# Where modulation sums and token sums stand in the engines' order, and the last down projection by latent then context columns

## The chip, the cores and the metric

One NeuronCore of a Trainium2 chip runs the whole program. The metric is the device time of one execution in microseconds (us): the median over the runs, and beside it the time of one execution recorded by the hardware profiler. The engines are TensorE (PE in the profile; PEld is its weight load), VectorE (DVE), ScalarE (ACT), GpSimd (POOL) and SyncE (SP), whose queue issues the transfers from memory. Each engine executes its instructions strictly in one order.

## The reference

A diffusion transformer with two layers, 512 latent tokens and 256 context tokens of width 1024. Each layer's norms are modulated by vectors that come from a condition: six chunks of 1024 for each layer, for latents and for context.

```python
for i in range(DEPTH):                       # 2
    mod_l = silu(c) @ ada_w[i] + ada_b[i]    # 6 x 1024: shift, scale, gate (mixer), shift, scale, gate (FFN)
    mod_c = silu(c_ctx) @ ada_w[i] + ada_b[i]
    hn = rms_norm(h, norm_mix_w[i]) * (1 + sc1) + sh1
    y = attention(hn) if i == 0 else hgrn2(hn)
    h = h + gt1 * y
    hn = rms_norm(h, norm_ffn_w[i]) * (1 + sc2) + sh2
    a, u = split(hn @ ffn_w_in[i])           # 1024 x 5632
    h = h + gt2 * ((silu(a) * u) @ ffn_w_out[i])     # 2816 x 1024
    # the context goes the same way, in layer 0 only; in layer 1 it only feeds the mixer
return rms_norm(h, final_norm_w)
```

Everything is float32.

## The kernel before, in words

**Tiling.** The tokens lie along the free dimension: `hT[k]`, k = 0 to 7, holds 128 features by 768 tokens, columns 0 to 511 latents and 512 to 767 context. A product of two float32 matrices is done as three matmuls of rounded parts, `mm3` (L113, L114, L115: high by high, high by low, low by high). So each operand is split first: `split` takes the high part on ACT (L89) and the low part on DVE (L92), unless another engine is named. Tiles of weights come through a ring of raw, high and low tiles; a load (L850 for the FFN) waits until a raw tile of the ring is free.

**Order.** The program text is Python that emits instructions; a scheduler then fixes the order of each engine by modelled readiness and cost. What an engine meets at run time is that fixed order, with waits on semaphores. All loads go through SP's one queue, in order too.

**Layer-0 FFN** (`ffn`, about 424 to 983 us in the profile). The hidden dimension is 22 tiles of 128. Tiles 0 and 1 are multiplied plainly, tiles 2 to 21 by a scheme that takes 7 instead of 8 block products over the two halves (384) of the token columns: the units m1, m2, m5, m6, m4, m3, m7 of `pair_units`. Their results are combined by DVE (L1008, L1035, L1043) and ACT (L1002, L1036). A product's PSUM bank is free for the next when its combination or copy has read it. The down projection is summed into `hT` in five parts of 5, 5, 4, 4, 4 hidden tiles, each with eight output tiles o (`fo_units`, `fo`). For each o there is a latent run (128x512) and a context run (128x256) of matmuls, and `residual` (L679, DVE) adds each run's bank, times its gate, to `hT`. In the last part `fo_out` also sums the squares of the new `hT` over k (`sumsq_add`: squares on ACT L270, additions on DVE L271) for the next norm. `LATE = 4`: for o of 4 and more of the last part the context runs are held back until all latent runs are done, and the weights of those o lie in tiles of their own (`fot1`, `fot3`). Between the context runs `norm_tail` makes the norm's factor for the latents: column sums on PE (L277), scale and power (L279 DVE, L281 POOL), and the broadcast (L287 DVE, L291 PE).

**Modulation sums.** `ada_acc` forms one chunk of the modulation as a matrix-vector product on DVE: for each half of 512 columns, eight loads of 128x512 weights (tile `adw`, L218), one product (L237) and seven accumulations (L239) by a column of the activated condition, for each of nv columns (2 with context, 1 without), then a transpose (L245) and a reduction (L246), and at the end a small matmul and addition (L253, L254). It is a generator: `fill.step(n)` takes it n yields further, so the place of the calls sets where in the program text its instructions stand. In the layer-0 FFN `ada_mix` runs chunks 0 and 1 of layer 1 (two steps after each down-projection unit); chunks 2, 3 and 4 run in the HGRN heads with `wide=True` (loads of two tiles at once, the sum in `acc_n`), one step at each scan step. Chunk 5 runs in the layer-1 FFN.

**Passage to the mixer.** `modulate` makes the normed and modulated tiles for k = 0 to 7, for the latents and, three k later, for the context: a DVE product with the norm's factor (L311) into a temporary `mtmp` (two buffers), the high part on ACT (L312), the low part on DVE for even k (L314), on ACT and POOL for odd k (L317). A copy of the scan masks (L1417, DVE) follows it.

**HGRN heads** (1012 to 1480 us). Each of eight heads runs projections (`hg`, `hz`, `hq`, `hv`) as fill between the steps of a log-depth scan (`scan_head`: L1481 and L1482 on POOL, L1504, L1534, L1541 on DVE, L1509, L1527 on PE). Then the layer-1 FFN, `ffn_plain`, runs to the end.

## Time and profile before

| | us |
|---|---|
| median of 3 runs | 1883.21 (1881.03 to 1883.71) |
| the profiled execution | 1879.18 |
| its span | 1877.3 |
| PE busy | 1792.3 (95%) |
| DVE busy | 1231.6 (66%) |
| ACT busy | 765.4 (41%) |
| POOL busy | 531.7 (28%) |

A row of the profile's groups gives line, engine, operation, output and inputs by the program's names, with the busy time and mean duration. A row of waits gives the engine and line that waited, whom it waited for, the total in us, the number of waits and the longest. In a row of the timeline the bracket at the end is the engine's idle time just before and what ended it. A row of busy time by stage gives the window, its length, and for PE, PEld, DVE, ACT and POOL the busy time with the number of instructions, then PE's granted clock, the share of the transfer engines and GB/s.

### The profile page before, as it was taken

The page shows a single profiled execution, that of the slowest core. Times are in us where ns is not written, and L with a number is a line of the kernel's source. Part 1 is how long each engine was busy: PE and PEld are TensorE (multiplying, and loading weights), DVE is VectorE, ACT ScalarE, POOL GpSimd, SP SyncE. Part 2 cuts the span into 40 slices and gives each one's busy share as a digit, 9 for nine tenths or more (in the row PEclk, how much of TensorE's full clock was granted, in tenths as well). Part 3 has the DMA queues.
Part 4 walks back from the last instruction along what each step waited for, and adds up shares of the span by engine and source line. Part 5 has one row for each costly group of instructions (what it writes and reads, how often), then busy time and mean ns, then how long its engine had stood idle before and what let it go on. Part 6 is the DMA issues. An engine that isn't in the chain of part 4 may idle for free.

```text
span 1877.3 us, 30240 instructions
## 1 busy us (share of the span) xinstructions
PE 1792.3 (95%) x11929; PEld 1632.8 (87%) x11929; DVE 1231.6 (66%) x2104; ACT 765.4 (41%) x1465; POOL 531.7 (28%) x501
## 2 busy tenths in 40 slices
PE   8989999999899999999999989999998999999998
PEld 6778688888789989999988889888897799898997
DVE  3676688888996646664676675676648774344443
ACT  4434777776433525252435233223233332232224
POOL 1244355445313313131314253434535200000000
PEclk9999999999999999999999999999999999999999
DMA  9433410002243122312232422232111243323331
GB/s 324 166 114 97 161 36 24 24 3 66 63 138 92 58 73 62 107 57 79 63 121 64 127 85 73 80 102 90 57 57 34 86 152 94 97 87 94 91 91 55
DMA packets 212942, 166.40 MB, mean 89 GB/s; under 512 B 7441, under 2 KB 189889, under 8 KB 212801
## 3 DMA queue, kind: packets, MB, share of 16 engines
q1 hardware_dynamic: 212512, 163.43, 28.5%
q8 instruction: 94, 1.54, 0.3%
q10 hardware_dynamic: 288, 1.05, 0.1%
q14 instruction: 48, 0.39, 0.1%
HBM read 162.36 MB, written 2.10 MB: 88 GB/s over the span
## 4 chain that ended last, share of the span: by engine, by line
PE 71%; DVE 15%; ACT 4%; DMA 4%; POOL 3%; issue 2%; SPq 0%; POOLq 0%; DVEq 0%; ACTq 0%
PE ffo L114 5%; PE ffo L115 5%; PE ffo L113 5%; PE ffi L113 4%; PE ffi L114 4%; PE ffi L115 4%; PE pt L706 3%; DMA adw<-in_ada_w_dram 2%; PE lv L1527 2%; PE x L115 2%; PE x L113 2%; PE x L114 2%; DVE QD L1534 2%; PE sc L648 2%; PE hz L114 1%
## 5 line engine op out<-in xcount | busy, mean ns | idle before, releaser
L114 PE MATMUL ffi<-fnl,whi_fi 128*128 128x256 f32 x704 | 198.0, 281 | 1.1 <-DVE fnl L1219 1.1
L113 PE MATMUL ffi<-fnh,whi_fi 128*128 128x256 f32 x704 | 198.8, 283 | 0.1
L115 PE MATMUL ffi<-fnh,wlo_fi 128*128 128x256 f32 x704 | 197.8, 281 | 0.0
L679 DVE SCALAR_TENSOR_TENSOR hT<-ffo,modc,hT 128x512 f32<-128x512 f32 (+1 forms) x106 | 66.8, 637 | 121.6 <-PE ffo L115 121.3
L114 PEld LDWEIGHTS ffi<-fnl,whi_fi 128*128 128x128 f32 x704 | 133.2, 189 | 1.7 <-DVE fnl L1219 1.5
L113 PEld LDWEIGHTS ffi<-fnh,whi_fi 128*128 128x128 f32 x704 | 132.7, 189 | 0.4 <-issue 0.3
L115 PEld LDWEIGHTS ffi<-fnh,wlo_fi 128*128 128x128 f32 x704 | 132.8, 189 | 0.0
L1534 POOL TENSOR_TENSOR KD<-KD,tot 128x384 f32<-128x384 f32 x96 | 106.2, 1130 | 75.5 <-ACT kc L1517 73.9
L281 POOL TENSOR_TENSOR rc<-rc,mhalf 128x2 f32<-128x2 f32 (+2 forms) x7 | 6.3, 902 | 395.9 <-DVE rc L279 395.9
L113 PE MATMUL ffo<-gh,whi_w 128*128 128x512 f32 (+1 forms) x320 | 107.6, 340 | 2.6 <-ACT gh L89 2.6
L696 POOL TENSOR_SCALAR pf<-pf,st 128x768 f32<-128x768 f32 (+1 forms) x96 | 73.6, 769 | 126.7 <-DVE st L695 90.2
L114 PE MATMUL ffo<-gl,whi_w 128*128 128x512 f32 (+1 forms) x320 | 108.7, 340 | 0.3 <-DVE gl L92 0.3
L115 PE MATMUL ffo<-gh,wlo_w 128*128 128x512 f32 (+1 forms) x320 | 108.9, 341 | 0.0
L89 ACT CAST whi_fi<-raw_fi 128x1024 fp32r<-128x1024 f32 x44 | 46.2, 1051 | 148.4 <-PE ffi L114 70.2
L1517 ACT COPY kc<-KD 128x256 f32<-128x256 f32 x112 | 42.8, 413 | 114.6 <-PE lv L1527 49.4
L92 DVE TENSOR_TENSOR ptl<-pt,pth 128x384 fp32r<-128x384 f32 (+1 forms) x160 | 79.8, 524 | 12.4 <-ACT pth L89 11.2
L89 ACT CAST pth<-pt 128x384 fp32r<-128x384 f32 (+1 forms) x160 | 69.9, 461 | 34.4 <-PE pt L706 22.7
L692 DVE TENSOR_REDUCE st<-sc 128x1 f32<-128x768 f32 (+1 forms) x96 | 74.2, 773 | 13.9 <-PE sc L649 11.1
L694 ACT ACTIVATE pf<-sc,st 128x768 f32<-128x768 f32 (+1 forms) x96 | 73.4, 765 | 19.2 <-DVE st L692 18.3
L113 PE MATMUL hz<-hnh,whi_hz 128*128 128x512 f32 (+1 forms) x224 | 78.6, 351 | 0.0
L1527 PE MATMUL lv<-QD,kc 128*128 128x128 f32 x448 | 65.2, 290 | 13.1 <-DVE QD L1534 8.9
L706 PE MATMUL pt<-ident,pf 128*128 128x128 f32 x448 | 72.2, 275 | 5.2 <-DVE ptl L92 3.9
(724 smaller groups left out, 5953.6 us busy)
## 6 DMA issues: line engine op xcount, KB each, us to landing
adw<-in_ada_w_dram SPq DMA_DIRECT2D x56, 512.0 KB, 4.0
raw_fi<-in_ffn_w_in_dram SPq DMA_DIRECT2D x44, 512.0 KB, 3.7
adw<-in_ada_w_dram SPq DMA_DIRECT2D x48, 256.0 KB, 2.9
raw_hz<-in_hgrn_w_in_dram SPq DMA_DIRECT2D x14, 512.0 KB, 3.8
raw_fo<-in_ffn_w_out_dram SPq DMA_DIRECT2D x16, 448.0 KB, 3.7
adr<-in_ada_w_dram SPq DMA_DIRECT2D x16, 256.0 KB, 4.4
adr<-in_ada_w_dram SPq DMA_DIRECT2D x8, 512.0 KB, 6.8
raw_wq<-in_attn_w_qkv_dram SPq DMA_DIRECT2D x8, 512.0 KB, 6.3
```

The costliest lines, as they stand in the source:

```text
L89: ACT.copy(hi, src)
L92: (eng or DVE).tensor_tensor(lo, src, hi.bitcast(F32), op=ALU.subtract)
L113: PE.matmul(ps, ahi, bhi, start=first, stop=False, **kw)
L114: PE.matmul(ps, ahi, blo, start=False, stop=False, **kw)
L115: PE.matmul(ps, alo, bhi, start=False, stop=last, **kw)
L679: DVE.scalar_tensor_tensor(hT[o][:, a:e], ps, mcol(layer, ch, o, v), hT[o][:, a:e], op0=ALU.mult, op1=ALU.add)
L692: DVE.tensor_reduce(st3[:, 0:1], ps[:, :nk], op=ALU.max, axis=AX.X, negate=True)
L694: ACT.activation(pf, ps[:, :nk], AF.Exp, bias=st3[:, 0:1], accum_out=st3[:, 1:2])
L696: POOL.tensor_scalar(pf, pf, st3[:, 2:3], 1.0, op0=ALU.mult, op1=ALU.mult)
L706: PE.transpose(pt[:, i * P : (i + 1) * P], pf[:, (i0 + i) * P : (i0 + i + 1) * P], ident)
L1527: PE.matmul(ps[:, cs], kc[:, cs], mv, start=True, stop=True)
L1534: eng.tensor_tensor(view, view, f, op=ALU.mult)
```

## The change

**Modulation sums.** In layer 0's FFN now chunks 0 to 3 are summed, in the HGRN heads only chunk 4, from head 1 on and at every third step. A narrow sum loads three tiles ahead (three buffers, before two); the yield that stood between a sum's first loads and its first product is gone; the transposed tile lies in the slot of `sw`. Steps are taken one at each pair unit m5 and three at each down-projection unit of parts 0 to 3 (before, two at each unit of all five parts and none at the pair units); for o > 0 two of the three stand between the latent and the context run. `pin` (`tc.keep_in_program_order`) holds the marked instructions of an engine in the order of the program text relative to their neighbours there: the products, accumulations and transposes of the sums, POOL's subtractions for the FFN's operands, and the masks copy.

**Last down projection.** All eight latent runs, then all eight context runs. The weights of o of 2 and more lie in tiles of their own. The squares are added on DVE for latents and on POOL for context. The norm's factor for the latents is made in the context runs of o = 2 and o = 4.

**Norm behind it.** The modulated tiles lie in slots that FFN operands left (`hnp`), and four temporaries (before, two) in the slot of one more operand; none of these slots is read by the last down projection. The masks copy stands behind the first pair of projections.

```diff
-LATE = 4
+    pin = tc.keep_in_program_order
-    def ada_acc(layer, ch, nv, fp, wide=False):
+    def ada_acc(layer, ch, nv, fp, wide):
...
-                raw = spare(f"adw{layer}{ch}{hf}{k}")
+                raw = fp.tile([P, 512], F32, tag="adraw", bufs=3, name=f"adw{layer}{ch}{hf}{k}")
...
-            raws = [load(hf, 0), load(hf, 1)]
-            yield
+            ahead = 2 if wide else 3
+            raws = [load(hf, i) for i in range(ahead)]
...
-                        DVE.scalar_tensor_tensor(a, raw, cc, a, op0=ALU.mult, op1=ALU.add)
-                    if v == nv - 1 and k + 2 < KT:
-                        raws.append(load(hf, k + 2))
+                        pin(DVE.scalar_tensor_tensor(a, raw, cc, a, op0=ALU.mult, op1=ALU.add))
+                    if v == nv - 1 and k + ahead < KT:
+                        raws.append(load(hf, k + ahead))
...
-            POOL.tensor_tensor(b11, b11, b12, op=ALU.subtract)
+            pin(POOL.tensor_tensor(b11, b11, b12, op=ALU.subtract))
...
-            POOL.tensor_tensor(b12, b22, b12, op=ALU.subtract)
+            pin(POOL.tensor_tensor(b12, b22, b12, op=ALU.subtract))
...
-                sumsq_add(acc_n[:, a:e], fp, hT[o][:, a:e], o, o == 0, tag="adraw", width=512)
+                sumsq_add(acc_n[:, a:e], late_pool[0], hT[o][:, a:e], o, o == 0, POOL if v else DVE,
+                          tag=f"g{8 + (o + v) % 2}", bufs=1, width=n)
...
-            if p_ == len(parts) - 1 and o >= LATE:
+            if p_ == len(parts) - 1:
                 held.append((o, g))
                 runs = [(o, g, spans[0])]
                 if o == KT - 1:
...
                 for (v, a, e), p in zip(spans, ps):
                     fo_out(p_, o, p, v, a, e)
+                fill.step(2)
                 return
             for (v, a, e), p in zip(spans, ps):
                 fo_mm(p_, g, p, a, e, range(nj))
                 fo_out(p_, o, p, v, a, e)
+                if v == 0:
+                    fill.step(2)
...
-                units.append(dict(own=None, w=512, after=after, src=src, pe=lambda g, fn=fn: fn(j, g), steps=0, done=done))
+                units.append(dict(own=None, w=512, after=after, src=src, pe=lambda g, fn=fn: fn(j, g), steps=int(i == 2), done=done))
...
-                if p_ == len(parts) - 1 and o >= LATE:
-                    own = ("t1", "t3")[(o - LATE) // 3], (o - LATE) % 3 * 512
+                if p_ == len(parts) - 1 and o >= 2:
+                    own = ("t1", "t3")[(o - 2) // 3], (o - 2) % 3 * 512
...
-                                  pe=lambda g, o=o: fo(p_, o, g), steps=2, done=("fo", p_, o)))
+                                  pe=lambda g, o=o: fo(p_, o, g), steps=int(p_ < len(parts) - 1), done=("fo", p_, o)))
...
-        for ch in range(2):
+        for ch in range(4):
             fill.add(ada_ffn(1, ch, fp))
...
-        if o == LATE + 1:
+        if o == 2:
             rst1.append(rstd_cols(fp, acc_n[:, :NL], NL))
-        elif o == KT - 1:
-            rst1[0] = rstd_psum(fp.tile([P, 512], F32, tag="adraw", bufs=2, name="dg"), rst1.pop(), NL)
+        elif o == 4:
+            rst1[0] = rstd_psum(fp.tile([P, T], F32, tag="g8", bufs=1, name="dg"), rst1.pop(), NL)
...
-    hi, lo = hn_tiles(hp)
+    hi, lo = [], []
+    for m in ("b11", "b21", "t4", "b22"):
+        for c, ts in (("h", hi), ("l", lo)):
+            t2 = hnp.tile([P, 2, T], F32R, tag=f"x{m}{c}", name=f"hn{m}{c}")
+            ts += [t2[:, 0], t2[:, 1]]
...
-    modulate(hp, hT, rst1, "mix", 1, hi, lo, SP2, ctx_rstd)
+    turns = [0]
+    mts = [hnp.tile([P, 2, T], F32, tag=f"xt2{c}", name=f"mt{c}") for c in "hl"]
...
+    modulate(mtmp, hT, rst1, "mix", 1, hi, lo, SP2, ctx_rstd)
...
-    DVE.tensor_copy(masks, mraw)
...
+    pin(DVE.tensor_copy(masks, mraw))
+    afill = Fill()
+    afill.add(ada_ffn(1, 4, hp, True))
     tail = None
-    afill = Fill()
-    for ch in (2, 3, 4):
-        afill.add(ada_ffn(1, ch, hp, True))
...
-            afill.step(1)
+            if h and i % 3 == 1:
+                afill.step(1)
...
-        if h == 1:
-            while len(afill.gens) > 2:
-                afill.step(1)
```

The lines of the changed kernel lie a little lower in number: L92 is L91 there, L239 is L235, L1035 is L1033, L1043 is L1041, L679 is L676. First DVE's order around the combination L1035 of hidden tile 3, at the start of the FFN; `adacc` is a modulation sum, `wlo_w` the low part of a weight tile. Before:

```order
L239 SCALAR_TENSOR_TENSOR adacc_6401<-adw_6537,csil,adacc_6401 128x512
L239 SCALAR_TENSOR_TENSOR adacc_6402<-adw_6537,csil,adacc_6402 128x512
L92 TENSOR_TENSOR wlo_w<-raw_('w', 3, 0)_5886,whi_w 128x512
L92 TENSOR_TENSOR wlo_w<-raw_('w', 3, 1)_5888,whi_w 128x512
L239 SCALAR_TENSOR_TENSOR adacc_6401<-adw_6581,csil,adacc_6401 128x512
L239 SCALAR_TENSOR_TENSOR adacc_6402<-adw_6581,csil,adacc_6402 128x512
L239 SCALAR_TENSOR_TENSOR adacc_6401<-adw_6630,csil,adacc_6401 128x512
L239 SCALAR_TENSOR_TENSOR adacc_6402<-adw_6630,csil,adacc_6402 128x512
L1035 TENSOR_TENSOR c_6015<-y,c_6015 128x384
```

Now:

```order
L1006 TENSOR_TENSOR c_5962<-z,c_5962 128x384
L91 TENSOR_TENSOR wlo_w<-raw_('w', 2, 0)_5885,whi_w 128x512
L91 TENSOR_TENSOR wlo_w<-raw_('w', 3, 0)_5889,whi_w 128x512
L233 TENSOR_SCALAR adacc_6007<-adw_6009,csil 128x512
L91 TENSOR_TENSOR wlo_w<-raw_('w', 3, 0)_5889,whi_w 128x512
L91 TENSOR_TENSOR wlo_w<-raw_('w', 3, 1)_5891,whi_w 128x512
L1033 TENSOR_TENSOR c_6028<-y,c_6028 128x384
```

The accumulations that stood ahead of the combination are gone from there; one first product is left.

Next DVE's order in part 2 of the down projection, units o = 0 to 2; before, there are no sums:

```order
L679 SCALAR_TENSOR_TENSOR hT_2004<-ffo,modc_82,hT_2004 128x512
L679 SCALAR_TENSOR_TENSOR hT_2004<-ffo,modc_82,hT_2004 128x256
L679 SCALAR_TENSOR_TENSOR hT_2005<-ffo,modc_82,hT_2005 128x512
L679 SCALAR_TENSOR_TENSOR hT_2005<-ffo,modc_82,hT_2005 128x256
L92 TENSOR_TENSOR wlo_w<-raw_('fo', 2, 6)_8292,whi_w 128x512
L92 TENSOR_TENSOR wlo_w<-raw_('fo', 2, 7)_8296,whi_w 128x512
```

Now:

```order
L676 SCALAR_TENSOR_TENSOR hT_2004<-ffo,modc_82,hT_2004 128x512
L676 SCALAR_TENSOR_TENSOR hT_2004<-ffo,modc_82,hT_2004 128x256
L235 SCALAR_TENSOR_TENSOR adacc_7840<-adw_7845,csil,adacc_7840 128x512
L235 SCALAR_TENSOR_TENSOR adacc_7839<-adw_7906,csil,adacc_7839 128x512
L235 SCALAR_TENSOR_TENSOR adacc_7840<-adw_7906,csil,adacc_7840 128x512
L676 SCALAR_TENSOR_TENSOR hT_2005<-ffo,modc_82,hT_2005 128x512
L235 SCALAR_TENSOR_TENSOR adacc_7839<-adw_8190,csil,adacc_7839 128x512
L235 SCALAR_TENSOR_TENSOR adacc_7840<-adw_8190,csil,adacc_7840 128x512
L676 SCALAR_TENSOR_TENSOR hT_2005<-ffo,modc_82,hT_2005 128x256
L91 TENSOR_TENSOR wlo_w<-raw_('fo', 2, 6)_8369,whi_w 128x512
L91 TENSOR_TENSOR wlo_w<-raw_('fo', 2, 7)_8373,whi_w 128x512
```

Three accumulations stand in each unit, among the residuals and the splits.

Last PE's order at the end of the down projection; `fot3` are the last weights, `rstd` the broadcast of the norm's factor, `h` the mixer's first projection. Before:

```order
L115 MATMUL ffo<-gh_10056,fot3l 128x256
L291 MATMUL rstd<-dg,ones 128x128 x4
L253 MATMUL adc_10374<-adpart_8493,fold 32x16 x4
L277 MATMUL ssq<-ones,acc_n 128x2 x2
L113 MATMUL h_10515<-hnh_10392,whi_h_10498 128x512
```

Now, first at the context run of o = 5, then at the run of o = 7:

```order
L114 MATMUL ffo<-gh_9923,fot3l 128x256
L288 MATMUL rstd<-dg,ones 128x128 x4
L112 MATMUL ffo<-gh_10068,fot3h 128x256
L113 MATMUL ffo<-gl_10069,fot3h 128x256
L114 MATMUL ffo<-gh_10068,fot3l 128x256
```

```order
L114 MATMUL ffo<-gh_10216,fot3l 128x256
L112 MATMUL h_10621<-hnb11h,whi_h_10604 128x512
L113 MATMUL h_10621<-hnb11l,whi_h_10604 128x512
L114 MATMUL h_10621<-hnb11h,wlo_h_10605 128x512
L112 MATMUL h_10622<-hnb11h,whi_h_10610 128x512
L274 MATMUL ssq<-ones,acc_n 128x2 x2
```

The broadcast has moved ahead by two context runs and a half, and the mixer's first matmul follows the last context matmul directly.

36 lines of the change are left out of this document (20 added, 16 removed).

## The prediction

> **What bounds the kernel now.** I read the page's chain first, then busy time by stage, then what TensorE (PE) waited for in the stages the change touches.
>
> ```profile
> span 1877.3 us, 30240 instructions
> PE 71%; DVE 15%; ACT 4%; DMA 4%; POOL 3%; issue 2%; SPq 0%; POOLq 0%; DVEq 0%; ACTq 0%
> ```
>
> ```profile
> 460.00:560.00 100.00, 89.83 (x484) 85.17 (x483) 94.35 (x148) 45.49 (x96) 32.14 (x24) 0.95 0.31 90
> 500.00:520.00 20.00, 16.02 (x80) 15.70 (x79) 20.00 (x27) 7.24 (x15) 7.29 (x6) 0.83 0.34 99
> 540.00:560.00 20.00, 18.01 (x92) 15.14 (x92) 17.52 (x31) 4.27 (x7) 0.00 (x0) 0.91 0.46 138
> 560.00:940.00 380.00, 380.00 (x2188) 362.52 (x2187) 237.05 (x363) 144.84 (x282) 95.05 (x68) 1.00 0.26 75
> 940.00:960.00 20.00, 19.07 (x106) 16.43 (x105) 16.06 (x25) 8.52 (x16) 2.39 (x1) 1.00 0.66 198
> 940.00:1020.00 80.00, 72.23 (x413) 61.70 (x412) 59.03 (x92) 35.66 (x60) 20.47 (x16) 0.98 0.29 89
> 1020.00:1300.00 280.00, 263.64 (x1809) 241.81 (x1808) 191.98 (x287) 86.59 (x171) 119.95 (x99) 0.98 0.32 96
> 1300.00:1420.00 120.00, 117.38 (x784) 106.64 (x783) 64.67 (x103) 37.32 (x68) 51.02 (x41) 1.00 0.18 54
> ```
>
> The columns are the window and its length, then busy time of PE, weight loads, DVE, ACT and POOL, the granted clock, the DMA share and GB/s. PE sets the end almost everywhere, so only its lost time can be won. I count that as window minus busy time times clock: 100 - 89.83 x 0.95 = 14.7 us at the start of the layer-0 FFN; nothing in its body; 80 - 72.23 x 0.98 = 9.2 us at the passage into the HGRN mixer; 280 - 263.64 x 0.98 = 21.6 us in the HGRN heads while modulation sums run there; 2.6 us in the 120 us after the sums are gone, 6.1 us at that rate for 280. What PE waited for, for the three stages in turn:
>
> ```profile
> PE x L113 <- ACT c L1002: 5.7, 2, 4.0
> ...
> PE h L114 <- POOL hnl L317: 2.7, 6, 0.8
> PE ssq L277 <- DVE acc_n L271: 2.5, 1, 2.5
> ...
> PE lv L1527 <- DVE QD L1534: 8.9, 9, 1.8
> PE lv L1509 <- DVE kfb L1504: 4.7, 2, 3.6
> PE hg L114 <- DVE wlo_hg L92: 2.8, 1, 2.8
> ```
>
> The releasers are DVE work, or work of ACT and POOL fed by DVE. So DVE's order is what matters, and that is what the change rewrites.
>
> **Start of the FFN: -10 us (bounds -13 and -4).** DVE is busy 94.35 of 100 us there. The largest PE gap:
>
> ```profile
> 498.92 5.85 DVE L239 SCALAR_TENSOR_TENSOR adacc<-adw,csil,adacc 128x512 f32<-128x512 f32 x4
> 505.89 3.77 DVE L239 SCALAR_TENSOR_TENSOR adacc<-adw,csil,adacc 128x512 f32<-128x512 f32 x4
> 509.58 0.54 DVE L1035 TENSOR_TENSOR c<-y,c 128x384 f32<-128x384 f32 x1
> 513.67 0.69 PE L113 MATMUL x<-xt2h,whi_w 128*128 128x384 f32 x1 [3.98 <-ACT c L1002]
> ```
>
> Eight sums, 5.85 + 3.77 = 9.62 us, stand ahead of the combination L1035, whose followers (L1043, L1044, the copy L1002) free the bank that PE waits for. In the new order one sum (a first product) stands in this stretch, so L1035 comes up to 9 us earlier and the 3.98 us gap closes; with it goes the clock, 0.83 in that slice: the slice loses 20 - 16.02 x 0.83 = 6.7 us, of which 2.7 is clock. The next slice of that kind, 540 to 560, loses 3.6 us, again with pairs of sums ahead of L1035. 6.7 + 3.6 = 10.3 us are what I see caused by sums. The other 4.4 us lie before 500, where DVE runs splits more than sums; POOL's subtractions, now pinned one block after the other, delay what DVE makes of the second block, and DVE stays nearly full. I take -10: a little of the 4.4 is won, a little of the 10.3 stays. The lower bound of gain, -4, is the one gap that certainly closes; -13 leaves under 2 us in the stretch.
>
> The Trainium skill (TensorE: Matmul & The Clock Gate, Part 1: The HAM clock gate) says that the array falls to half clock only after an idle window of about 3.4 us. The 3.98 us gap with 0.83 agrees. The slice 540 to 560, where PE was idle for 20 - 18.01 = 2 us in all and the clock still fell to 0.91, does not. By the rule only the first dip could go with its gap; by the rows both do, 1.6 us more (18.01 x 0.09), and the rows decide.
>
> **Body of the FFN: +2 us (bounds 0 and +8).** Two more chunks, 2 and 3 of layer 1, are summed here, each for latents alone. Prices:
>
> ```profile
> L239 DVE SCALAR_TENSOR_TENSOR adacc<-adw,csil,adacc x70: 731/744/1782, 480.3 to 1532.3; 128x512 f32<-128x512 f32 x70
> L237 DVE TENSOR_SCALAR adacc<-adw,csil x10: 475/484/1520, 471.8 to 1515.0; 128x512 f32<-128x512 f32 x10
> L245 DVE STREAM_TRANSPOSE adt<-adacc x10: 669/702/712, 517.0 to 1533.1; 128x512 f32<-128x512 f32 x10
> ```
>
> A half chunk is one product, seven sums, a transpose and a reduction (taken like the transpose): 0.48 + 7 x 0.744 + 2 x 0.70 = 7.1 us; four halves 28 us. Some 13 products and sums pushed out of the start add 10 us. DVE idles 380 - 237 = 143 us in the body, so 38 us fit on the mean. They are not spread evenly, though: each down-projection unit of parts 0 to 3 now carries three steps.
>
> ```profile
> 870.84 0.75 DVE L679 SCALAR_TENSOR_TENSOR hT<-ffo,modc,hT 128x512 f32<-128x512 f32 x1 [0.91 <-PE ffo L115]
> 872.25 0.48 DVE L679 SCALAR_TENSOR_TENSOR hT<-ffo,modc,hT 128x256 f32<-128x256 f32 x1 [0.67 <-PE ffo L115]
> 875.04 0.75 DVE L679 SCALAR_TENSOR_TENSOR hT<-ffo,modc,hT 128x512 f32<-128x512 f32 x1 [2.31 <-PE ffo L115]
> 853.07 0.68 DVE L92 TENSOR_TENSOR wlo_w<-raw_('fo', 3, 4)_9116,whi_w 128x512 fp32r<-128x512 f32 x1
> ```
>
> PE gives a unit every 875.04 - 870.84 = 4.20 us, 1.41 of it context. DVE then needs 0.75 + 0.48 + 0.68 + 3 x 0.744 = 4.14 us: at par, with nothing to spare. Cover for lateness is the six PSUM banks that the runs take in turn, two to a unit: three units, about 12 us. And each pinned sum now waits in DVE's order for its load, which goes through SP's queue:
>
> ```profile
> SPq L850 <- DVE wlo_w L92: 327.1, 63, 24.2
> ...
> DVE hT L679 <- PE ffo L115: 48.7, 44, 2.3
> ```
>
> ```profile
> adw<-in_ada_w_dram SPq DMA_DIRECT2D x9, 256.0 KB, 2.9
> ```
>
> SP spends 327 of the body's 380 us held by weight loads that wait for a free buffer; a modulation load issued behind one comes late, and lands 2.9 us after its issue. Behind the waiting sum stand DVE's residual updates and weight splits, for which PE waits next. Three buffers ahead and one unit (4.2 us) between reuse make 2.9 us coverable. By counting steps (36 for each chunk with two columns, 18 with one; one a pair tile and three a unit), chunks 0 and 1 end in the middle of part 2, and the 12 units from there to the end of part 3 work on one column, where each sum takes a load of its own. Three loads and one weight tile are 1 MB in 4.2 us, 250 GB/s; 198 GB/s took a 0.66 share between 940 and 960, so this is 0.83, below full. I take 2 us, near nothing, as PE never stalled here in 380 us; 8 is two thirds of a microsecond at each of the 12 units.
>
> **Passage into the mixer: -7 us (bounds -9 and -2).** Rows of POOL and of DVE there:
>
> ```profile
> 962.90 2.93 POOL L92 TENSOR_TENSOR wlo_h<-raw_h,whi_h 128x1024 fp32r<-128x1024 f32 x1 [6.19 <-ACT whi_h L89]
> 979.59 1.13 POOL L281 TENSOR_TENSOR rc<-rc,mhalf 128x4 f32<-128x4 f32 x1 [13.75 <-DVE rc L279]
> ```
>
> ```profile
> 963.49 2.63 DVE L271 TENSOR_TENSOR acc_n<-acc_n,sq 128x256 f32<-128x256 f32 x1
> ...
> 979.42 0.41 DVE L271 TENSOR_TENSOR acc_n<-acc_n,sq 128x256 f32<-128x256 f32 x1
> ...
> 984.46 0.17 DVE L254 TENSOR_TENSOR modc<-adc,cols 128x16 f32<-128x16 f32 x1 [0.63 <-PE adc L253]
> ```
>
> Now all eight latent runs come before the eight context runs; the context runs, 8 x 1.41 = 11.3 us of PE, cover the latent norm. After the last latent run stand a residual (0.75), a square and its addition (taken like the residual, 1.5), the column sums, POOL's power (1.13) and the broadcast, some 6 us with what is queued between, and then the first modulated tile (three operations like the residual, about 2): below 11.3. The ssq wait of 2.5 us goes, the scale that comes late (its addition L254 runs at 984.46) goes, the masks cast no longer stands among the norm's operations. The waits for hnl (2.7 us, POOL) go in part, as eight tiles are started behind context matmuls. Left over: about 2 us, for the first rstd behind POOL or for hnl. 9.2 - 2 = 7. The least gain, 2, is the ssq wait alone; the most is everything.
>
> The context's squares are now added on POOL. The same rows show what DVE and POOL do to each other: an addition of 128x256, 0.41 us at 979.42, took 2.63 at 963.49 beside POOL's split of 962.90. Seven POOL additions can cost DVE several microseconds in the worst case; this is why I don't take -9. The Trainium skill (SBUF — State Buffer, Who interferes with whom) says it as a rule: a DVE instruction with two SBUF inputs and a GpSimd instruction that reads SBUF take turns on a shared port for whole instructions. The 2.63 us agrees; the rule speaks against this part of the change.
>
> **HGRN heads: -12 us (bounds -15.5 and -6).** Two of three chunks leave, the third is started in head 1 and stepped every third step.
>
> ```profile
> L239 DVE SCALAR_TENSOR_TENSOR acc_n<-adw,csil,acc_n 128x512 f32<-128x512 f32 x41 | 34.1, 832 | 13.0 <-DMA adw<-in_ada_w_dram 12.3
> ```
>
> ```profile
> DVE acc_n L237 <- DMA adw<-in_ada_w_dram: 9.7, 5, 3.3
> ```
>
> ```profile
> 1034.00 1.54 DVE L239 SCALAR_TENSOR_TENSOR acc_n<-adw,csil,acc_n 128x512 f32<-128x512 f32 x2 [3.51 <-DMA adw<-in_ada_w_dram]
> 1035.46 1.22 DVE L92 TENSOR_TENSOR wlo_hg<-raw_hg,whi_hg 128x1024 fp32r<-128x1024 f32 x1
> ```
>
> ```profile
> 1036.73 0.38 PE L114 MATMUL hg<-wlo_hg,hnh 128*128 128x256 f32 x1 [2.81 <-DVE wlo_hg L92]
> ```
>
> DVE stood 12.3 + 9.7 = 22 us for modulation loads here, and worked 34 us on the sums. The second group shows how that reaches PE: the sum waits 3.51 us, the split behind it is late, PE waits 2.81. The stretch lost 21.6 us against 6.1 at the later rate: 15.5 us can be laid to three chunks. A third of that for the one left is 5, but at three times the spacing its loads should land in time, so I leave 3.5: -12. The least, -6, counts only what I can follow to a sum: the wlo_hg wait (2.8) and one kfb wait (3.6).
>
> **Sum.** -10 + 2 - 7 - 12 = -27 us. The profiled execution took 1879.2 us (span 1877.3), 4 us below the median of the runs, 1883.2. So about 1852 profiled and **1856 us** as a median. All bounds at once give -38 to -4, medians 1845 to 1879.
>
> **Rivals.** (1) DVE stays the bound of the FFN's start, since splits and POOL keep it full whichever sums go: for it, 94.35 of 100 us busy; against it, the 9.62 us of sums right ahead of the gap. With -2, +4, -5 and -9: -12, 1871. (2) The waits in the heads are those of the scan's own chain (QD, kfb behind POOL), and the sums only filled idle DVE: for it, QD is the largest wait, 8.9 us; against it, the loss falls to 2.6 us in 120 once the sums end. With -4, +6, -2 and -3: -3, 1880, no change. (3) Slower: in the 12 one-column units the loads, held behind weight loads in SP's queue, come one after another instead of three at a time. A unit then lasts 3 x 2.9 = 8.7 us against 4.2: 12 x 4.5 = 54, less 12 of cover, 42 us; with the other terms' -29, +13, 1896. It decides for slower from (29 + 4 + 12) / 12 = 3.8 us lost a unit. For it: SP's 327 us of waits, DVE at par, sums that can no longer be passed; against: three loads ahead, and 250 GB/s is within what was moved. (4) All gains in full: -38, 1845. That the change doesn't do what it says (sums left over at the FFN's end) is excluded by the order: the last of chunk 3 stands ahead of the last projection.
>
> **Chances.** Forecast 0.60, its own range 1848 to 1866; rival 1 0.17; rival 2 0.07; rival 3 0.08; full gain 0.08. A change within 0.2% (3.8 us) can't be told from none. Faster: 0.60 + 0.17 + 0.08 = 0.85; same 0.07; slower 0.08. The range, from just below the full gain to between rivals 1 and 2, is 1843 to 1877.
>
> **What would show it.** Right: PE busy near 100 of 100 with clock 1.00 from 500 to 560; no PE wait on acc_n at the passage; DMA waits of DVE below 5 us in the heads. Wrong: PE idle in the body, released by L92 or L679 behind a DVE wait for adw; QD and kfb waits as before in the heads; an rstd wait above 2 us at the passage. The forecast fails as a whole if PE's gaps keep their length with the sums gone from in front of them.

## The result, and the profile after

The changed kernel takes 1858.22 us (median of 4 runs, 1857.14 to 1858.52) against 1882.3 us before (with one run more than the 1883.21 above): ratio 0.987, 95% interval 0.985 to 0.989, 24 us less. The forecast was 1856, range 1843 to 1877. The profiled execution took 1857.14 us.

The page of the changed kernel, its span and the engines' shares of the chain:

```profile
span 1855.4 us, 30297 instructions
PE 80%; DVE 9%; POOL 4%; ACT 4%; issue 2%; DMA 1%; POOLq 0%; SPq 0%; DVEq 0%; ACTq 0%
```

DVE's share of the chain fell from 15 to 9% and that of transfers from 4 to 1%. To see where, I cut both executions at the same instructions of PE and took busy time by stage. The six stages are: the attention's output projection, the plain tiles of the layer-0 FFN (to the first m1), pair tiles 2 to 4 (to the first down projection), the FFN's body (to the last product of tile 21), the last down projection with the mixer's first projection, and the heads (from the first scan matmul to the layer-1 FFN). Before:

```profile
424.80:444.79 19.99, 18.79 (x110) 17.90 (x109) 15.98 (x35) 10.55 (x20) 8.73 (x8) 1.00 0.18 53
444.79:485.95 41.16, 37.18 (x206) 34.27 (x206) 38.66 (x66) 29.27 (x64) 24.20 (x21) 1.00 0.15 46
485.95:538.90 52.95, 46.77 (x253) 45.82 (x253) 51.08 (x76) 22.87 (x47) 14.74 (x10) 0.94 0.36 106
538.90:942.90 404.00, 402.01 (x2300) 381.48 (x2300) 258.04 (x398) 150.34 (x292) 95.05 (x68) 1.00 0.27 79
942.90:1013.92 71.02, 63.25 (x346) 52.72 (x345) 52.81 (x83) 30.74 (x52) 15.86 (x12) 0.98 0.26 80
1031.32:1484.42 453.10, 425.35 (x2850) 383.86 (x2849) 300.31 (x465) 144.35 (x280) 188.97 (x161) 0.99 0.26 77
```

After, the same six stages, and behind them the two slices of 20 us that the prediction shows of before:

```profile
426.81:448.85 22.04, 19.10 (x111) 17.87 (x110) 17.42 (x35) 10.56 (x20) 8.69 (x8) 1.00 0.26 84
448.85:492.33 43.48, 38.23 (x205) 35.66 (x205) 35.11 (x66) 29.63 (x64) 19.98 (x19) 0.96 0.09 25
492.33:540.69 48.36, 45.89 (x253) 45.22 (x253) 33.99 (x50) 23.94 (x48) 18.06 (x12) 0.96 0.21 62
540.69:941.02 400.33, 400.33 (x2324) 380.00 (x2324) 312.37 (x476) 149.77 (x290) 105.46 (x68) 1.00 0.37 110
941.02:1006.83 65.81, 61.40 (x337) 52.35 (x337) 38.70 (x64) 31.98 (x53) 20.56 (x20) 0.97 0.21 66
1024.23:1462.94 438.71, 421.28 (x2835) 381.45 (x2833) 271.88 (x429) 144.35 (x280) 186.21 (x161) 1.00 0.21 64
...
500.00:520.00 20.00, 18.52 (x97) 18.52 (x98) 15.68 (x27) 11.07 (x23) 6.73 (x5) 0.91 0.29 86
540.00:560.00 20.00, 20.00 (x112) 17.38 (x112) 15.51 (x26) 3.85 (x6) 0.00 (x0) 1.00 0.46 136
```

By stage: +2.0 in the output projection, +2.3 in the plain tiles, -4.6 in the pair tiles, -3.7 in the body (the stall at its first down projection; PE is now busy for all of it, with DVE at 312 of 400 us), -5.2 at the passage, -14.4 in the heads. DVE is down from 51 of 53 us to 34 of 48 in the pair tiles, where its order was full. The attention took 424.8 us before and 426.8 after. Nothing was changed there, and over the 14 profiles of this study it varied from 424.3 to 427.0, so those 2 us are scatter; the layer-1 FFN gave 0.4. The sum, +2.0 + 2.0 + 2.3 - 4.6 - 3.7 - 5.2 - 14.4 - 0.4, is the 21.9 us between the spans.

What PE waited for in the changed kernel, at the FFN's start, at the passage and in the heads:

```profile
PE ffi L113 <- DVE xb22l L91: 3.3, 1, 3.3
PE x L112 <- ACT c L1000: 2.0, 1, 2.0
...
PE rstd L288 <- DVE dg L284: 1.6, 1, 1.6
PE ssq L274 <- POOL acc_n L268: 1.4, 1, 1.4
...
PE lv L1523 <- DVE kfb L1518: 4.7, 2, 3.7
PE lv L1541 <- DVE QD L1548: 3.4, 5, 1.5
```

The waits for the bank of `x` fell from 5.7 to 2.0 us. Of the 5.7, the 3.98 us behind the combination, before hidden tile 3's m6, are gone. (The combination itself is hidden tile 2's; the section on the change calls it tile 3's.) The 2.0 us left are the other wait, 1.67 us before, at hidden tile 2's m6, ahead of any combination: ACT's copy of the bank stands behind a cast for which ACT idled 5.69 us, until POOL had added up blocks of weights. This wait, and the dip of the clock behind it, are the 0.91 in the slice 500 to 520. The waits for QD fell from 8.9 to 3.4, and `wlo_hg` is gone. The wait for `xb22l` grew from 0.9 to 3.3 us, and two waits at the passage are new, both behind POOL's additions. The kfb wait is what it was.

### The profile page after: what moved, and what is told of

Its sections match the earlier page's. It is cut to its first block, busy times and chain, and to the rows that moved or that the text cites. A ratio compares the mean times of both kernels' runs of the same rounds, so it can differ in the third digit from the quotient of the medians.

```text
span 1855.4 us, 30297 instructions
## 1 busy us (share of the span) xinstructions
PE 1787.0 (96%) x11929; PEld 1630.3 (88%) x11929; DVE 1219.8 (66%) x2097; ACT 766.8 (41%) x1465; POOL 542.2 (29%) x508
## 3 DMA queue, kind: packets, MB, share of 16 engines
q10 hardware_dynamic: 288, 1.05, 0.1%
## 4 chain that ended last, share of the span: by engine, by line
PE 80%; DVE 9%; POOL 4%; ACT 4%; issue 2%; DMA 1%; POOLq 0%; SPq 0%; DVEq 0%; ACTq 0%
PE ffo L112 5%; PE ffo L113 5%; PE ffo L114 5%; PE ffi L112 4%; PE ffi L113 4%; PE ffi L114 4%; PE pt L703 3%; PE x L112 2%; PE x L113 2%; PE x L114 2%; PE lv L1541 2%; PE hz L112 2%; PE hz L113 2%; PE hz L114 2%; PE y L114 1%
## 5 line engine op out<-in xcount | busy, mean ns | idle before, releaser
L676 DVE SCALAR_TENSOR_TENSOR hT<-ffo,modc,hT 128x512 f32<-128x512 f32 (+1 forms) x106 | 66.9, 635 | 90.9 <-PE ffo L114 90.9
L1548 POOL TENSOR_TENSOR KD<-KD,tot 128x384 f32<-128x384 f32 x96 | 101.3, 1078 | 68.2 <-ACT kc L1531 66.6
L114 PE MATMUL ffo<-gh,wlo_w 128*128 128x512 f32 (+1 forms) x304 | 102.6, 338 | 0.0
L113 PE MATMUL ffo<-gl,whi_w 128*128 128x512 f32 (+1 forms) x304 | 102.4, 337 | 0.0
L112 PE MATMUL ffo<-gh,whi_w 128*128 128x512 f32 (+1 forms) x304 | 101.7, 337 | 0.0
L91 DVE TENSOR_TENSOR ptl<-pt,pth 128x384 fp32r<-128x384 f32 (+1 forms) x160 | 79.8, 523 | 12.4 <-ACT pth L88 11.2
L235 DVE SCALAR_TENSOR_TENSOR adacc<-adw,csil,adacc 128x512 f32<-128x512 f32 x98 | 81.6, 846 | 2.6 <-DMA adw<-in_ada_w_dram 1.9
L1548 DVE TENSOR_TENSOR QD<-QD,tot 128x256 f32<-128x256 f32 x96 | 55.5, 618 | 41.2 <-PE lv L1541 40.5
```

Source lines behind the costliest of these rows:

```text
L91: (eng or DVE).tensor_tensor(lo, src, hi.bitcast(F32), op=ALU.subtract)
L112: PE.matmul(ps, ahi, bhi, start=first, stop=False, **kw)
L113: PE.matmul(ps, ahi, blo, start=False, stop=False, **kw)
L114: PE.matmul(ps, alo, bhi, start=False, stop=last, **kw)
L235: pin(DVE.scalar_tensor_tensor(a, raw, cc, a, op0=ALU.mult, op1=ALU.add))
L676: DVE.scalar_tensor_tensor(hT[o][:, a:e], ps, mcol(layer, ch, o, v), hT[o][:, a:e], op0=ALU.mult, op1=ALU.add)
```

## The experiments

Stage lengths in us, as cut above, from one profile each, beside the median of the runs. "Passage" is the last down projection with the mixer's first projection.

| kernel | median | attention | output proj. | plain tiles | pair tiles | body | passage | heads |
|---|---|---|---|---|---|---|---|---|
| before | 1882.3 | 424.8 | 20.0 | 41.2 | 53.0 | 404.0 | 71.0 | 453.1 |
| the change | 1858.2 | 426.8 | 22.0 | 43.5 | 48.4 | 400.3 | 65.8 | 438.7 |
| sums not pinned | 1876.7 | 425.9 | 23.4 | 36.5 | 58.5 | 405.3 | 65.8 | 443.0 |
| POOL not pinned | 1852.1 | 425.1 | 23.6 | 40.5 | 45.8 | 400.3 | 66.8 | 438.7 |
| chunks 2, 3 in heads | 1865.4 | 426.7 | 22.0 | 42.2 | 48.1 | 399.6 | 65.3 | 448.9 |
| chunk 4 dense | 1856.5 | 424.9 | 22.0 | 44.8 | 45.5 | 400.3 | 65.3 | 440.1 |
| run order undone | 1855.8 | 426.0 | 22.0 | 44.7 | 45.6 | 400.3 | 66.0 | 438.8 |
| sums in last part | 1861.5 | 425.3 | 23.4 | 43.7 | 48.1 | 404.2 | 66.5 | 440.0 |
| context on DVE | 1854.2 | 425.9 | 22.1 | 44.7 | 45.6 | 400.3 | 63.4 | 440.0 |
| w01 back | 1853.9 | 424.3 | 20.0 | 42.4 | 49.5 | 400.0 | 65.3 | 438.7 |
| one load ahead | 1857.8 | 426.5 | 23.5 | 43.7 | 48.1 | 400.3 | 65.8 | 438.7 |
| two edits | 1850.3 | 427.0 | 23.6 | 40.5 | 45.8 | 400.3 | 63.4 | 438.7 |
| three edits | 1849.2 | 426.6 | 20.0 | 40.5 | 48.1 | 400.0 | 63.4 | 440.0 |
| four edits | 1855.1 | 426.6 | 20.0 | 40.6 | 46.6 | 407.1 | 63.4 | 438.6 |

Plain and pair tiles are to be read together where the order of the first m1 shifts (36.5 + 58.5). The output projection, the plain tiles, the pair tiles and the heads also step by 1.2 to 2.8 us in kernels whose edit doesn't touch them. The pair tiles' 48.4 and 45.6 are one order of instructions: where they take 45.6, the clock dips twice in the plain tiles, which then take 44.7, and not once in each, so that the two stages together differ by 1.5 us. The kernel before, run beside each set of experiments, had medians from 1880.6 to 1882.3. So a median that moves by less than 3 us is judged by the stage that the edit touches.

### Sums not pinned

```diff
-                        pin(DVE.tensor_scalar(a, raw, cc, None, op0=ALU.mult))
+                        DVE.tensor_scalar(a, raw, cc, None, op0=ALU.mult)
...
-                        pin(DVE.scalar_tensor_tensor(a, raw, cc, a, op0=ALU.mult, op1=ALU.add))
+                        DVE.scalar_tensor_tensor(a, raw, cc, a, op0=ALU.mult, op1=ALU.add)
...
-                pin(DVE.transpose(turned, a))
+                DVE.transpose(turned, a)
```

> The changed kernel with one edit: products, accumulations and transposes of the modulation sums are not held in the order of the text; the table of steps, three loads ahead and the number of chunks stay. In this order nine or ten accumulations again stand ahead of the combination of hidden tile 3. Theory A (the pinning, not the table of steps, closed the gap at the FFN's start, since only pinned sums stay where the text has them): PE waits 3 to 4 us again before hidden tile 3, the clock there falls below 0.9, and waits appear at the down projections where accumulations are drawn ahead: +6 to +10 us, 1864 to 1868. Rival B (three loads ahead and the steps at the pair tiles spread the sums enough): within 2 us of 1858.

Measured: 1876.7 us, +18.5, more than Theory A's 10; the ratio to before is 0.998 (0.997 to 0.999). Three quarters of the gain are lost without the pins. DVE's timeline around the combination of hidden tile 2, without them:

```profile
503.78 5.84 DVE L235 SCALAR_TENSOR_TENSOR adacc<-adw,csil,adacc 128x512 f32<-128x512 f32 x4
...
512.51 2.06 DVE L235 SCALAR_TENSOR_TENSOR adacc<-adw,csil,adacc 128x512 f32<-128x512 f32 x3
514.50 0.54 DVE L1033 TENSOR_TENSOR c<-y,c 128x384 f32<-128x384 f32 x1
```

and PE's waits at the FFN's start in the same execution:

```profile
PE x L112 <- ACT c L1000: 5.4, 2, 3.4
PE x L114 <- DVE wlo_w L91: 3.4, 1, 3.4
```

The picture of before comes back: the same 5.84 us of four accumulations ahead of the combination, and 5.4 us of waiting for the bank, of which 3.4 stand before tile 3's m6 again. With the same table of steps and the same loads ahead, the scheduler draws the sums forward to where their loads are ready. The loss is not there alone: +3.1 in plain and pair tiles together, +4.9 in the body, +4.3 in the heads, +3.7 in the layer-1 FFN, whose chunk 5 is pinned by the same lines. These 3.7 us are no gain undone, for the change had won only 0.4 there: without pins that stage takes 396.1 us, against 392.9 before the change.

### POOL not pinned

```diff
-            pin(POOL.tensor_tensor(b11, b11, b12, op=ALU.subtract))
+            POOL.tensor_tensor(b11, b11, b12, op=ALU.subtract)
...
-            pin(POOL.tensor_tensor(b12, b22, b12, op=ALU.subtract))
+            POOL.tensor_tensor(b12, b22, b12, op=ALU.subtract)
```

> The changed kernel with one edit: POOL's subtractions for the operands t1 and t3 are no longer held in the order of the text (first all four of t1, then all four of t3). The scheduler then alternates them, and DVE's difference L983 no longer stands ahead of xb22l with only a t3 subtraction to release it late. Theory A (the 3.3 us wait of PE for xb22l at 478 us is the price of that pinning; DVE stood 3.83 us before L983 for POOL L971): the wait falls to about 1 us, as before the change, and the time to about 1855.5 (1858.2 - 2.5). Rival B (the wait comes from DVE and POOL sharing the stretch, whatever their order, and only its name changes): the stretch between the first FFN matmul and the first product m1 keeps its 43.5 us, time 1858.

Measured: 1852.05 us, -6.2. In the changed kernel POOL's timeline and DVE's have the wait at the plain tiles' end (L967 makes t1, L971 t3):

```profile
472.50 4.25 POOL L967 TENSOR_TENSOR x<-x 128x384 f32<-128x384 f32 x4
476.71 4.51 POOL L971 TENSOR_TENSOR x<-x,x 128x384 f32<-128x384 f32 x4
...
477.76 1.35 DVE L983 SCALAR_TENSOR_TENSOR x<-x,x 128x384 f32<-128x384 f32 x1 [3.83 <-POOL x L971]
```

Pinned, POOL finishes all four subtractions of t1 before the first of t3, and L983, which needs the first of t3, stands in DVE's order ahead of `xb22l`. Without the pin PE's wait for `xb22l` is

```profile
PE ffi L113 <- DVE xb22l L91: 0.4, 1, 0.4
```

0.4 us, and the plain tiles take 40.5 us against 43.5. Theory A holds, with 3.0 us in its stage. Another 2.6 in its profile are the pair tiles', 1.0 of it less waiting and the rest a dip of the clock that isn't there.

### Chunks 2 and 3 in the heads again

```diff
-        for ch in range(4):
+        for ch in range(2):
             fill.add(ada_ffn(1, ch, fp))
...
-    afill.add(ada_ffn(1, 4, hp, True))
+    for ch in (2, 3, 4):
+        afill.add(ada_ffn(1, ch, hp, True))
...
-            if h and i % 3 == 1:
-                afill.step(1)
+            afill.step(1)
...
+        if h == 1:
+            while len(afill.gens) > 2:
+                afill.step(1)
```

> The changed kernel with one part undone: chunks 2 and 3 are summed in the HGRN heads again, with chunk 4, one step at each scan step from head 0, as in the kernel before; all else stays. Theory A (the move out of the heads is worth what the heads gained, about 14 us between the mixer's first projection and the layer-1 FFN, and costs nothing in the FFN's body): +12 to +15 us, 1870 to 1873, with DVE waiting some 20 us for modulation loads in the heads and PE for wlo_hg and QD. Rival B (most of the heads' gain came from the passage, hn tiles in other slots, masks copy moved): +4 us or less, below 1862.

Measured: 1865.4 us, +7.2, between the two. The heads take 10.2 us more, the body 0.7 and the passage 0.5 less: this is the price of the two chunks at the one place and at the other. The groups of DVE from 1020 to 1300 us and PE's waits there:

```profile
L235 DVE SCALAR_TENSOR_TENSOR acc_n<-adw,csil,acc_n 128x512 f32<-128x512 f32 x42 | 39.2, 934 | 0.1
```

```profile
PE lv L1541 <- DVE QD L1548: 4.2, 1, 4.2
PE lv L1523 <- DVE kfb L1518: 3.7, 2, 2.2
PE hg L113 <- DVE wlo_hg L91: 3.0, 3, 1.6
```

Theory A named the wrong cause. DVE stood 22 us for loads of these sums before; here 0.1 us, and the heads are still 10 us longer. PE idles 23.4 us in the heads, against 17.4 in the change, and the rest goes with the granted clock, 0.98 against 1.00. What is left as a cause is DVE's time itself, 39 us at a mean of 934 ns, in front of the scan's QD and the splits; that is read from the waits, not tested apart. The other 4 us of the heads' 14.4 are not in the move of the chunks. The run without pins lost 4.3 us in the heads with one chunk there, so the pins are the nearest cause; masks copy and new slots were not told apart from them.

### Chunk 4 dense

```diff
-            if h and i % 3 == 1:
-                afill.step(1)
+            afill.step(1)
```

> The changed kernel with one edit: chunk 4's sum takes one step at each scan step from head 0 on, not every third step from head 1 on; chunks 2 and 3 stay in the FFN. Theory A (the heads lost by sums that came faster than their loads of 4 us, so spacing is part of the gain): DVE waits for loads in heads 0 and 1, PE for wlo_hg or QD behind them, +3 to +5 us, 1861 to 1863. Rival B (the heads lost by the amount of the sums; one chunk is harmless at any rate): within 1.5 us of 1858.

Measured: 1856.5 us (1854.8 to 1861.3); the heads take 1.4 us more than with the spread sum, which they also do in kernels that leave them alone, and no load is waited for. Rival B: for one chunk the rate does not count.

### Run order undone

```diff
-            if p_ == len(parts) - 1:
+            if p_ == len(parts) - 1 and o >= 4:
                 held.append((o, g))
...
-                if p_ == len(parts) - 1 and o >= 2:
-                    own = ("t1", "t3")[(o - 2) // 3], (o - 2) % 3 * 512
+                if p_ == len(parts) - 1 and o >= 4:
+                    own = ("t1", "t3")[(o - 4) // 3], (o - 4) % 3 * 512
...
-        if o == 2:
+        if o == 5:
...
-        elif o == 4:
+        elif o == KT - 1:
```

> The changed kernel with one part undone: in the last down projection outputs 0 to 3 take their latent and context runs together and only outputs 4 to 7 hold the context back, and the norm's factor is made at context outputs 5 and 7, as before; the squares of the context stay on POOL, the norm's slots and temporaries stay. Theory A (cover: eight context runs, 11.3 us, hide the norm's start, four, 5.7 us, do not): the wait before the norm's column sums or factor comes back, some 3 to 5 us in all with the clock, 1861 to 1863. Rival B (the passage gained by the finished scale, the freed DVE and the slots, not by the run order): within 1 us of 1858.

Measured: 1855.8 us (1853.7 to 1861.8). The passage takes 66.0 us against 65.8, so Theory A falls: four context runs cover as much as eight. PE's waits are the same two, and a third for the high part of the last hidden tile:

```profile
PE rstd L288 <- DVE dg L284: 1.4, 1, 1.4
PE ssq L274 <- POOL acc_n L268: 1.4, 1, 1.4
PE ffo L112 <- ACT gh L88: 1.4, 1, 1.4
```

In the change the rest of the waiting is 0.7 us for `hnb22l`, a low part made on POOL, and 0.7 for a residual on `hT`; in all it is 4.4 us there and 4.2 here.

### Sums in the last part

```diff
-                units.append(dict(own=None, w=512, after=after, src=src, pe=lambda g, fn=fn: fn(j, g), steps=int(i == 2), done=done))
+                units.append(dict(own=None, w=512, after=after, src=src, pe=lambda g, fn=fn: fn(j, g), steps=0, done=done))
...
-                                  pe=lambda g, o=o: fo(p_, o, g), steps=int(p_ < len(parts) - 1), done=("fo", p_, o)))
+                                  pe=lambda g, o=o: fo(p_, o, g), steps=1 if p_ < len(parts) - 1 else 2, done=("fo", p_, o)))
```

> The changed kernel with other places for the steps: none at the pair tiles, two at each unit of the last down projection, so that a dozen accumulations and the transposes stand among its latent runs; chunks, pins and run order stay. Theory A (the passage to the mixer gained because the modulation sums no longer stand in the last down projection, where they took DVE's time ahead of residuals, squares and factor; the run order is not what won it): +3 to +5 us, 1861 to 1863, lost between the last part and the mixer's first projection. Rival B (eight context runs of 11.3 us cover the norm whatever DVE does in the latent runs): within 1.5 us of 1858.

Measured: 1861.5 us, +3.3, the size that Theory A gave, but not at its place. PE's waits in the body and at the passage:

```profile
PE adc L250 <- DVE adpart L243: 2.7, 1, 2.7
...
PE ssq L274 <- DVE acc_n L268: 2.4, 1, 2.4
```

The ssq wait of before (2.5 us) is back, so the sums did cause it; yet the passage takes 66.5 us, 0.7 more than in the change, as other waits shrank. The loss is in the body, 3.9 us (2.7 of waiting and a dip of the clock behind it), at a small matmul of PE that I had not considered: `adc`, which closes a chunk, stands in PE's order, and PE waits there for the chunk's last reduction on DVE.

With either the run order or the sums' absence undone the passage keeps 4.5 to 5 of its 5.2 us. So each alone is enough, or the slots and temporaries of the norm did it; a kernel without both was not run, and this stays open.

### Context's squares on DVE

```diff
-            sumsq_add(acc_n[:, a:e], late_pool[0], hT[o][:, a:e], o, o == 0, POOL if v else DVE,
+            sumsq_add(acc_n[:, a:e], late_pool[0], hT[o][:, a:e], o, o == 0, DVE,
```

> The changed kernel with one edit: the context's squares in the last down projection are added on DVE, not on POOL. Theory A (what is left of the passage's loss comes from POOL: the broadcast's operand waits for a slot that a POOL addition frees, PE 1.6 us at rstd, and the context's column sums wait for POOL's last addition, PE 1.4 us): both waits go, -2 to -3 us, 1855 to 1856. Rival B (DVE, with eight more additions of 0.41 us beside the residuals and the norm, becomes late instead): the waits move to hn tiles on DVE, 1858 or up to 1860.

Measured: 1854.2 us, -4.0; the passage 63.4 us against 65.8. PE's waits there:

```profile
PE rstd L288 <- DVE dg L284: 1.2, 1, 1.2
PE h L112 <- DVE hT L676: 0.9, 1, 0.9
PE ssq L274 <- DVE acc_n L268: 0.4, 1, 0.4
```

Theory A by the size, 2.4 us in the stage, and by half of its mechanism. The wait at the column sums falls by 1.0; the factor's only from 1.6 to 1.2, so the slot behind POOL was a small part of it. In all PE waits 3.2 us against 4.4, and the other half of the 2.4 us is a dip of the clock that isn't there: the granted clock of the stage is 1.00, in the change 0.97. The remaining 1.6 of the median are what plain and pair tiles, in an unchanged order, gave in this profile (90.3 us against 91.8).

### w01 back in the FFN's pool

```diff
-                hnp.tile([P, 4 * H], F32R, tag=f"xt2{c}", name=f"w01{c}")[:, 0:1024] for c in "hl"]
+                fp.tile([P, 4 * H], F32R, tag=f"xt1{c}", name=f"w01{c}")[:, 0:1024] for c in "hl"]
```

> The changed kernel with one edit: the split of the plain FFN weight w01 lies in a slot of the FFN's own pool again (that of operand t1) and not in the norm's slots, which are free earlier. In ACT's order the cast of the attention output o then stands ahead of the cast w01h again. Theory A (the 2 us that the changed kernel loses in the attention's output projection come from that cast: it comes 1 us earlier than o's, and POOL's split behind it falls on DVE's split of o, which took 2.50 us against 0.96 before): that stretch falls from 22.0 to 20 us, 1856. Rival B (the 2 us are another order of PE's matmuls there, or scatter): within 0.7 us of 1858.

Measured: 1853.9 us, -4.4; the output projection takes 20.0 us again, as before the change. DVE's split of the attention's output, in the changed kernel, with POOL's row beside it, and then with this edit:

```profile
429.21 2.50 DVE L91 TENSOR_TENSOR o<-ofp,o 128x768 fp32r<-128x768 f32 x1 [1.38 <-ACT o L88]
...
428.53 2.37 POOL L91 TENSOR_TENSOR w01l<-raw_('w', 0, 1)_5304,w01h 128x1024 fp32r<-128x1024 f32 x1 [2.63 <-ACT w01h L88]
```

```profile
426.23 0.96 DVE L91 TENSOR_TENSOR o<-ofp,o 128x768 fp32r<-128x768 f32 x1 [0.90 <-ACT o L88]
```

Theory A. The cast of w01 had slipped ahead of that of `o` on ACT because its slot came free earlier; POOL's split behind it fell on DVE's, and one instruction took 2.50 us where it takes 0.96. This is the contention that the Trainium skill (SBUF — State Buffer, Who interferes with whom) describes, at a place where I had not looked, since the change moves nothing there by intent. The gain beyond 2 us is in the attention's scatter.

### One load ahead

```diff
-            ahead = 2 if wide else 3
+            ahead = 2 if wide else 1
```

> The changed kernel with one size changed: a narrow modulation sum loads one tile ahead and not three. Theory A (the pinned sums in the FFN's body are safe only because three loads are under way: with one, each sum waits for most of a load, 2.9 us, and DVE has nothing to spare in the down-projection units): PE idles at the down projections of parts 1 to 3, +20 to +60 us, 1878 to 1918. Rival B (six banks and the split weights cover it, DVE catches up in the pair tiles): below +5 us, 1863 at most.

Measured: 1857.8 us, no change, body 400.3 us. DVE's wait for these loads in the body, with one ahead:

```profile
DVE adacc L235 <- DMA adw<-in_ada_w_dram: 1.7, 3, 0.9
```

In the change it is 1.9 us. The run decides nothing between the theories, because the edit did not take hold: the three buffers stayed, and in the two traces every engine, SP's queue included, has the same instructions in the same order, with the sums' loads issued at the same distance from the first FFN matmul to 0.1 us. The size of `ahead` only says where in the program text a load stands, and the loads are not pinned. So whether three loads ahead are needed stays open; a run with one buffer instead of three would have asked it. What the run gives is a repeat of the change, 1857.8 beside 1858.2 us, whose output projection took 23.5 us against 22.0 with nothing changed.

### Two, three and four edits

The three edits that gained (POOL not pinned, context on DVE, w01 back) together; the fourth sums chunk 4 in the FFN as well:

```diff
-        for ch in range(4):
+        for ch in range(5):
...
-    afill.add(ada_ffn(1, 4, hp, True))
...
-                units.append(dict(own=None, w=512, after=after, src=src, pe=lambda g, fn=fn: fn(j, g), steps=int(i == 2), done=done))
+                units.append(dict(own=None, w=512, after=after, src=src, pe=lambda g, fn=fn: fn(j, g), steps=int(i in (2, 5)), done=done))
```

> The changed kernel with two edits together that were faster alone: POOL's subtractions not held in the text's order (-6.2 us of median alone) and the context's squares added on DVE (-4.0 alone). Theory A (two separate waits, xb22l and the factor's slot with the column sums, each with its own price): the sum, -10, 1848. Rival B (both runs alone also lost the same dip of the clock after m1, 2.7 us in the stretch from m1 to the first down projection, 45.6 to 45.8 us against 48.4, which can be won once): -7.5, 1850.5 to 1851.

> The kernel of the two edits with w01 back in the FFN's own pool as well. Theory A (the 2 us in the attention's output projection are separate from the rest): 2 us below the kernel with two edits, 1846 to 1849. Rival B (w01 in t1's slot makes the splits of t1 late, as the 3.2 us gap after m5 in the run with that edit alone suggests, and gives the 2 us back): no better than the two edits.

> The kernel of the three edits with chunk 4 summed in the layer-0 FFN too, one more step at each pair tile, so that no sums are left in the HGRN heads. Theory A (the FFN's body has room on DVE for 14 us more, since two chunks there cost under 1 us and one load ahead cost nothing, and the heads still pay a little for the spread chunk): -1 to 0 us beside the three edits. Rival B (the pair tiles' combinations and splits come late behind two steps a tile): +3 us or more, PE idle in the body. In the heads no difference above 1 us is expected from either, so a larger gain would say that even the spread chunk cost something there.

Measured: 1850.3, 1849.2 and 1855.1 us. The two edits gain 7.9 together, not 10.2: Rival B, what plain and pair tiles give can be won once. The third takes its gain in the output projection (23.6, of which 1.5 is a dip of the clock, and 20.0). It loses 2.3 in the pair tiles, and not at an unchanged order: in DVE's order the splits of t1 now stand behind those of t3 and t2, PE waits 2.1 us against 1.5, and the clock dips. This is what its Rival B feared, in part; the medians differ by 1.1, so neither theory is decided. The fourth loses 5.9: its body takes 407.1 us. PE's wait in the body, and busy time around it:

```profile
PE adc L250 <- DVE adpart L243: 4.0, 2, 3.3
```

```profile
770.00:790.00 20.00, 16.70 (x92) 14.88 (x91) 18.15 (x28) 2.28 (x4) 5.20 (x4) 0.86 0.47 143
```

Rival B, by the same closing matmul as above, not by splits or combinations: 4.0 us of waiting, and the clock at 0.86 makes them 7.1. The heads take 438.6 us without a sum, and 438.7 in the change with one, so the last sum cost nothing there. The kernel with three edits is the best that ran: ratio to before 0.9825 (0.981 to 0.984), 9 us below the change.

## Why the prediction was right, and where it was not

The total, -27 forecast and -24 measured, is right, and in part by luck. The start of the FFN and the passage gave 5.8 us less than forecast, body and heads 4.4 more, and 2 us that no term held were lost ahead of them. The reasons are only partly right. Of the signs that the prediction named, DVE's waits for loads are gone from the heads and PE does not idle in the body; but PE still waits at the context's column sums, the slice 500 to 520 has a clock of 0.91, and the kfb wait is as before.

**FFN's start, -10 forecast.** Measured -6.0: +2.3, -4.6, and -3.7 for the stall at the first down projection. The mechanism, sums ahead of L1035, was right: the gap of 3.98 us behind it is gone, and the run without pins brings 3.4 us of it back. The step that was mis-sized is the half sentence on POOL's pinned subtractions: I named them and charged nothing for them, and they cost 3.0 us plus the chance of a clock dip. With POOL not pinned the same three stages give -11.6 against before (40.5 + 45.8 + 400.3 against 41.2 + 53.0 + 404.0).

**Not in the sum at all: +2 in the output projection,** from moving w01 to another pool. I had read the order only at the places that the change names.

**Body, +2 forecast.** Measured 0 (PE busy 400.33 of 400.33 us), inside the bounds. The danger I described, loads late in SP's queue (rival 3), is not there with three buffers: DVE waited 1.9 us for the sums' loads in the whole body. The danger that exists is another, PE's closing matmul `adc`, and it decides as soon as the steps are placed otherwise (+3.9 and +7.1 us in two kernels). My list of who waits behind a late sum had residuals and splits, and left out the instruction that the sum itself issues on PE.

**Passage, -7 forecast.** Measured -5.2. The waits that I expected to go (ssq, the late scale, part of hnl) went; the cause that I gave, eight context runs as cover, was not shown: with four the passage is as short. The step that was mis-sized is the rest, left at 2 us: PE still waits 4.4 us, 1.6 at rstd, 1.4 at the context's column sums, 0.7 each for `hnb22l` and `hT`, and the clock of the stage is 0.97. The waiting fell by 3.4 us, from 7.8; the other 1.8 of the 5.2 is time in which PE counts as busy (63.25 and 61.40 us), which was not followed. POOL's additions, which I feared for DVE, cost PE through the column sums.

**Heads, -12 forecast.** Measured -14.4. Of this 10 are the two chunks, as the run with them put back shows. But the step "DVE stood 22 us for modulation loads here", from which I took how the loss reaches PE and the hope in the spacing, failed: with the waits gone and the chunks present the 10 us are still lost. And the 3.6 us kfb wait that I laid to a sum is no sum's: in the kernel with four edits, which has no sums in the heads, it is still there.

```profile
PE lv L1523 <- DVE kfb L1518: 3.5, 1, 3.5
```

The pins were what the prediction spoke of least. Without them 18.5 us are lost, 3.7 of them in the layer-1 FFN, where the change had little to win. This does not add up with the 10 us of the two chunks: each is the loss when one part is taken away from the whole change.

## What to carry to other kernels

Filler work on a shared engine costs by how much of it there is and where it stands in that engine's order, even when its data is never late. A table that spaces the work does little while the scheduler may draw it forward (without pins the whole change kept 5.6 of its 24 us). After an experiment's edit, compare the order of the engines first: an edit of the text that leaves the order alone has tested nothing. When a stage of filler is moved, list every instruction that it issues on every engine, the small closing one on the bottleneck above all, and compare the whole order, also at places that the edit doesn't name. Pin only what is filler: the same pin on work that feeds the path cost 3 us here.
